# Both output projections of a hybrid decoder kernel by seven half-size block products (one level of Strassen)

## The chip, the cores and the metric

One core of one Trainium2 chip runs the whole program in one launch. The metric is device time in microseconds of that core; a profiled execution also gives a span from the first to the last instruction, which is a little shorter than its time. TensorE is called PE, VectorE DVE, ScalarE ACT, GpSimd POOL and SyncE SP; SP computes nothing here and only issues DMAs, in order.

## The reference, cut to what matters

Two layers work on x of 1024 tokens by 1024 channels. Each makes a y of 1024 tokens by 2048 channels and ends in an output projection with a 2048 by 1024 weight matrix, added to x:

```python
# layer 0 (even): two branches, concatenated to 2048 channels
y_a = u * sg.reshape(bsz, seq, A_WIDTH) * jax.nn.silu(za)
...
return jnp.concatenate([y_a, y_b], axis=-1) @ w_out
# layer 1 (odd): attention over 16 heads, 2048 channels
o = o.reshape(bsz, seq, C_WIDTH) * jax.nn.silu(z)
return o @ w_out
# trunk
x = x + even_layer(...); x = x + odd_layer(...)
return rmsnorm(x, final_g)
```

## The kernel before

All products keep float32 accuracy by splitting both operands: `split2` makes a high part in fp32r (ACT casts it) and a low part (DVE subtracts), and each block product is three matmuls, high-high, high-low and low-high. `fetch_w` loads a weight chunk of 128 by 1024 (512 KB) on SP's queue into one of two buffers `wr`, `split_w` makes `wh` and `wl` of it, also two buffers each.

The order of the program: normalisation and gates; the gMLP stage (`gmlp`), in which group after group g = 0 to 7 takes a `u` weight chunk, 48 matmuls of 128x512 and eight small `sp` matmuls, and then eight `za` groups of 48 matmuls; the mLSTM heads (`mlstm`); the output projection of layer 0; the second layer's attention, 16 heads; the output projection of layer 1; the final normalisation. The finished gMLP rows `yu` go to DRAM (`yd`) from POOL's queue. A Tile scheduler orders each engine's instructions from this program, with its buffers and their reuse; each queue then runs in its own order.

An output projection has 16 blocks of 128 channels (kb) by 8 tiles of 128 tokens. y comes from DRAM (`yd` in layer 0, `wd` in layer 1, where it is multiplied by `rr`, the rows of inverse norms, first) into `wout_y`. Columns 0 to 511 are made first in eight PSUM tiles, two from `unit` (named un) and six named wps, by 128x512 matmuls: 16 x 8 x 3 = 384 a layer. Then `wout_rest` makes columns 512 to 767 and 768 to 1023, each by 384 matmuls of 128x256, while the earlier columns are added to the residual `xa`, squared for the norm (ACT) and multiplied by the gain `gB` (POOL, L344). The last piece is finished tile by tile.

`split_w` waits for a free pair wh, wl, so a weight load on SP can wait until PE has read the weights two chunks earlier; what stands behind it on SP waits too. In layer 1 the loads of y and rr stand on the same queue, and rr goes through two buffers `yr` that DVE must have read.

Of the kernel before, what the change touches and what calls it, by code (L numbers as in the profile page):

```python
# [35 lines left out]

Y0, PA = 4, 2
# [9 lines left out]
class Trunk:  # L47
# [106 lines left out]
    def run(self):  # L154
        tc, nc, io = self.tc, self.nc, self.io
        with tc.tile_pool(name="const", bufs=1) as cp, \
# [6 lines left out]
            self.x2 = dp.tile([NT, P, D], F32, name="x2d")  # L163
            self.wp = tc.alloc_tile_pool(name="weights", bufs=1)
# [8 lines left out]
            run(self.wout_part(range(2, 8), 0, Y0))  # L173
# [4 lines left out]
            q = pool("wout0c")  # L178
            self.wout_y(q, Y0, 8, wy)
            self.wout_y(p, 8, 16, wy)  # L180
            run(self.wout_part(range(8), Y0, 16))
            rest = self.wout_rest(p)
            next(rest)
            q.release()
            wy.release()

# [4 lines left out]
            for t in range(NT):  # L191
                next(rest)
                if t >= 2:
                    self.to_feature(self.xa[t - 2], t - 2, *((self.psum, "S", 2) if t >= 6 else ()))
            ps = [self.unit() for _ in range(2)]
            self.proj_half(w, ps[0], 0)
            self.to_feature(self.xa[6], 6, self.psum, "C", 2)
# [7 lines left out]
            self.to_feature(self.xa[7], 7, self.psum, "C", 2)  # L205
# [11 lines left out]
            for h in range(CH):  # L217
                att = self.odd_head(odd, h)
                for i in range(NT):
                    if i in SLOTS.get(h, range(NT)):  # L220
                        next(fill, None)
                        left -= 1
                        if left == 0:
                            hT.release()
                            wy = pool("wout1a")
                            self.wout_start(1)
                            self.wout_y(wy, 0, PA, wy)
                            self.wout_ps(range(2))
                            fill = self.wout_part(range(2), 0, PA)
                    next(att)  # L230
            self.odd_tail(odd, CH - 1)
            run(fill)
            self.wout_y(wy, PA, 7, wy)
            self.wout_ps(range(2, 8))
            run(self.wout_part(range(2, 8), 0, PA))
            run(self.wout_part(range(8), PA, 7))
# [18 lines left out]
    def wout_start(self, layer):  # L255
        self.layer = layer
        self.yh, self.yl, self.ysplit = [], [], []
        self.wsrc = self.io["wF"] if layer == 0 else self.io["wG"]
        self.wps = [None] * NT

    def wout_ps(self, ts_):

        t1 = lambda tag, n=1, w=512: self.psum.tile([P, w], F32, name="wps", tag=tag, bufs=n)
        for t in ts_:
            if t < 2:
                self.wps[t] = self.unit()
            elif self.layer == 0:
                self.wps[t] = t1(*{2: ("S", 2), 3: ("S", 2), 4: ("C", 2), 5: ("C", 2), 6: ("N",), 7: ("o",)}[t])
            elif t >= 6:
                self.wps[t] = t1("tp" if t == 6 else "O")  # L270
            elif t % 2 == 0:
                two = t1("S", 2, T)
                self.wps[t], self.wps[t + 1] = two[:, :512], two[:, 512:]

    def wout_y(self, pool, lo, hi, raws):

        nc = self.nc
        if self.layer == 1 and raws is pool:
            pool.tile([P, T], F32, name="yr", tag="yr", bufs=2)
        for kb in range(lo, hi):  # L280
            self.yh.append(pool.tile([P, T], F32R, name=f"yh{kb}"))
            self.yl.append(pool.tile([P, T], F32R, name=f"yl{kb}"))
        for kb in range(lo, hi):
            raw = self.yl[kb].bitcast(F32)
            ld = nc.sync.dma_start(out=raw, in_=(self.y if self.layer == 0 else self.w)[kb])
            if self.layer == 1:
                o, raw = raw, raws.tile([P, T], F32, name="yr", tag="yr", bufs=2)
                nc.sync.dma_start(out=raw, in_=self.rr[kb:kb + 1].broadcast_to([P, T]))
                nc.vector.tensor_tensor(out=raw, in0=o, in1=raw, op=ALU.mult)
            self.ysplit.append((ld.ins, *self.split2(self.yh[kb], self.yl[kb], raw)))  # L290

    def wout_mm(self, ps, kb, t, wh, wl):
        sl = slice(t * P, (t + 1) * P)
        for n, (a, b) in enumerate(((self.yh, wh), (self.yh, wl), (self.yl, wh))):
            self.nc.tensor.matmul(out=ps, lhsT=a[kb][:, sl], rhs=b, start=(kb == 0 and n == 0), stop=(kb == 15 and n == 2))  # L295

    def wout_part(self, ts_, lo, hi):

        for i in range(lo // 2, (hi + 1) // 2):
            w = self.fetch_w(self.wsrc[i])  # L300
            with self.after(*(self.ysplit[2 * i - 1][1:] if i else ())):
                wh, wl = (a.rearrange("p (k c) -> p k c", k=2) for a in self.split_w(w))
            for kb in range(max(lo, 2 * i), min(hi, 2 * i + 2)):
                for t in ts_:
                    self.wout_mm(self.wps[t], kb, t, wh[:, kb % 2, :], wl[:, kb % 2, :])
                yield
# [913 lines left out]
```

## Time and profile before

| what | value |
|---|---|
| median of 3 runs | 2156.04 us (2155.82 to 2158.85) |
| the profiled execution | 2155.46 us |
| its span | 2153.7 us |
| PE busy | 2122.1 us (99%) |
| DVE, ACT, POOL busy | 1375.5, 943.5, 188.7 us |
| DMA moved | 233.65 MB, mean 108 GB/s |
| mean granted clock of PE | 0.997 |

The time of a run is the span and 1.76 us around it. PE has work nearly all the time, so the time goes where PE's instructions go, and what another engine or queue does counts when PE then waits. The rows that matter stand further down.

### The profile page before, as it was taken

Reading aid. Unit: us, or ns where it says so; the run is one execution under the profiler, and the core shown is the slowest. Engines: PE = TensorE matmul, PEld = TensorE weight load, DVE = VectorE, ACT = ScalarE, POOL = GpSimd, SP = SyncE. Lnnn points to the kernel's source line nnn. Section 1 sums busy time; section 2 is a strip of 40 time slices with the busy share of each in tenths; the row PEclk is TensorE's granted clock in tenths of the full one; section 3 lists DMA queues with packets and bytes.
Section 4 is the critical chain, followed back from the end, with each engine's and each line's share of the span. In section 5 each row is a group of like instructions: output and inputs, shape, how many; then the busy total and the mean of one; then the engine's idle time right before and its main releaser. Section 6 shows DMA issues by size and latency. Waiting matters only on the chain.

```text
span 2153.7 us, 33782 instructions
## 1 busy us (share of the span) xinstructions
PE 2122.1 (99%) x12554; PEld 1858.8 (86%) x12554; DVE 1375.5 (64%) x3117; ACT 943.5 (44%) x1907; POOL 188.7 (9%) x315
## 2 busy tenths in 40 slices
PE   8899999999999999999999999999999999998998
PEld 7888889898989889988888888888888888887898
DVE  6352225767677622648777777777877777898525
ACT  5511214343434312335555555555555555665222
POOL 0000000000000000301111111110111011111002
PEclk9999999999999999999999999999999999999999
DMA  4311222111122441255444444444444443336812
GB/s 172 118 40 40 71 87 74 50 64 64 54 70 99 163 170 69 97 144 135 126 111 110 112 112 125 117 109 112 110 112 121 125 108 105 104 85 217 301 50 89
DMA packets 89337, 233.65 MB, mean 108 GB/s; under 512 B 19109, under 2 KB 20037, under 8 KB 89173
## 3 DMA queue, kind: packets, MB, share of 16 engines
q1 hardware_dynamic: 74420, 194.65, 29.7%
q0 software_dynamic: 14752, 36.85, 5.6%
q8 instruction: 99, 1.62, 0.3%
q14 instruction: 66, 0.53, 0.1%
HBM read 136.86 MB, written 27.43 MB: 76 GB/s over the span
## 4 chain that ended last, share of the span: by engine, by line
PE 84%; DVE 5%; DMA 3%; issue 3%; ACT 2%; SPq 2%; POOL 1%; DVEq 0%; POOLq 0%; ACTq 0%
PE un L135 38%; PE wps L295 11%; PE un L150 5%; PE S L558 5%; PE ops L150 4%; PE un L295 3%; PE O L604 3%; PE tp L590 3%; PE xps L135 2%; PE N L941 1%; PE O L605 1%; DMA sw<-xs 1%; PE vps L913 1%; PE dC L941 1%; SPq L451 1%
## 5 line engine op out<-in xcount | busy, mean ns | idle before, releaser
L135 PE MATMUL un<-hh,wh 128*128 128x512 f32 x1240 | 490.2, 395 | 1.2 <-ACT xs L437 1.2
L135 PE MATMUL un<-hh,wl 128*128 128x512 f32 x1240 | 490.2, 396 | 1.0 <-DVE wl L97 0.9
L135 PE MATMUL un<-hl,wh 128*128 128x512 f32 x1240 | 486.9, 393 | 0.0
L97 DVE TENSOR_TENSOR wl<-wr,wh 128x1024 fp32r<-128x1024 f32 (+1 forms) x163 | 205.4, 1261 | 315.2 <-ACT wh L96 283.6
L96 ACT CAST wh<-wr 128x1024 fp32r<-128x1024 f32 (+1 forms) x163 | 170.8, 1049 | 384.5 <-PE un L135 178.0
L135 PEld LDWEIGHTS un<-hh,wl 128*128 128x128 f32 x1240 | 233.0, 188 | 52.2 <-DVE wl L97 3.4
L135 PEld LDWEIGHTS un<-hh,wh 128*128 128x128 f32 x1240 | 233.4, 188 | 46.9 <-ACT xs L437 1.5
L135 PEld LDWEIGHTS un<-hl,wh 128*128 128x128 f32 x1240 | 233.1, 188 | 47.3
L566 ACT ACTIVATE p<-p,mn 128x128 f32<-128x128 f32 (+7 forms) x256 | 197.8, 774 | 122.7 <-DVE mn L563 122.5
L563 DVE CUSTOM_DVE_ANT_0 p<-S,mask 128x128 f32<-128x128 f32 (+7 forms) x256 | 184.9, 751 | 2.2 <-PE tp L590 1.7
L295 PE MATMUL wps<-wh,yh 128*128 128x256 f32 (+1 forms) x576 | 184.2, 321 | 0.2 <-ACT wps L323 0.2
L295 PE MATMUL wps<-wl,yh 128*128 128x256 f32 (+1 forms) x576 | 183.4, 319 | 0.0
L295 PE MATMUL wps<-wh,yl 128*128 128x256 f32 (+1 forms) x576 | 183.4, 319 | 0.0
L150 PE MATMUL un<-wh,hh 128*128 128x256 f32 (+1 forms) x560 | 160.3, 287 | 4.1 <-ACT wh L96 2.6
L150 PE MATMUL un<-wl,hh 128*128 128x256 f32 (+1 forms) x560 | 159.4, 285 | 1.4 <-DVE wl L97 1.4
L150 PE MATMUL un<-wh,hl 128*128 128x256 f32 (+1 forms) x560 | 159.2, 284 | 0.2 <-DVE hl L97 0.2
L97 DVE TENSOR_TENSOR PT<-tp,PT 128x512 fp32r<-128x512 f32 (+1 forms) x192 | 106.1, 553 | 30.4 <-ACT PT L96 30.2
L295 PEld LDWEIGHTS wps<-wh,yh 128*128 128x128 f32 x576 | 109.2, 190 | 9.4 <-ACT wps L323 0.8
L295 PEld LDWEIGHTS wps<-wh,yl 128*128 128x128 f32 x576 | 109.3, 190 | 7.6
L295 PEld LDWEIGHTS wps<-wl,yh 128*128 128x128 f32 x576 | 109.4, 190 | 7.4
L604 PE MATMUL O<-PT,Vh 128*128 128x512 f32 x320 | 113.6, 388 | 0.1
L96 ACT CAST PT<-tp 128x512 fp32r<-128x512 f32 (+1 forms) x192 | 91.6, 477 | 47.4 <-PE tp L590 44.9
(324 smaller groups left out, 4393.5 us busy)
## 6 DMA issues: line engine op xcount, KB each, us to landing
wr<-wO SPq DMA_DIRECT2D x79, 512.0 KB
wr<-wE SPq DMA_DIRECT2D x46, 512.0 KB
sw<-xs SPq DMA_DIRECT2D x256, 64.0 KB
Qh<-xh SPq DMA_DIRECT2D x128, 128.0 KB
Ql<-xl POOLq DMA_DIRECT2D x128, 128.0 KB, 4.0
wr<-wF SPq DMA_DIRECT2D x18, 512.0 KB
wr<-wG SPq DMA_DIRECT2D x18, 512.0 KB
yl<-yd SPq DMA_DIRECT2D x16, 512.0 KB
```

What stands on the lines that cost most here:

```text
L96: return (self.nc.scalar.copy(out=out_h, in_=src).ins, self.nc.vector.tensor_tensor(out=out_l, in0=src, in1=out_h.bitcast(F32), op=ALU.sub ...
L97: self.nc.vector.tensor_tensor(out=out_l, in0=src, in1=out_h.bitcast(F32), op=ALU.subtract).ins)
L135: nc.tensor.matmul(out=ps, lhsT=a[:, kb, :], rhs=b[:, kb, :], start=(kb == 0 and i == 0), stop=(kb == KB - 1 and i == 2))
L150: nc.tensor.matmul(out=ps, lhsT=a[:, k0 + k, sl], rhs=b, start=start and k == i == 0, stop=stop and k == n - 1 and i == 2)
L295: self.nc.tensor.matmul(out=ps, lhsT=a[kb][:, sl], rhs=b, start=(kb == 0 and n == 0), stop=(kb == 15 and n == 2))
L451: q.dma_start(out=dst[a:a + 64].bitcast(F32), in_=src[64 * c:64 * c + 64].bitcast(F32))
L558: mm(out=Ss[c][:, lo:lo + n], lhsT=Q2[c][qt // 4][i][:, qs], rhs=K2[c][lo // 512][:, :n], start=i == 0, stop=i == 1)
L563: nc.vector.tensor_tensor_reduce(out=p[:, :W], in0=S[:, :W], in1=self.mask[:, T - W:], scale=-0.125, scalar=1e30, op0=ALU.add, op1=ALU.min ...
L566: nc.scalar.activation(out=p[:, :W], in_=p[:, :W], func=AF.Exp, scale=-1.0, bias=mn, accum_out=s)
L590: self.nc.tensor.transpose(out=tp[:, i, :], in_=p[:, s0:s0 + P], identity=self.ident)
L604: mm(out=O.rearrange("p (a t) -> p a t", a=2)[:, :, a0:], lhsT=Vh, rhs=pt, start=s == 0, stop=False)
L941: mm(out=out, lhsT=lhsT[a], rhs=rhs[b], start=first and i == 0, stop=last and i == 2)
```

## The change

Both projections are made with 2 by 2 blocks: y in four blocks of 512 tokens by 1024 channels, the weights in four blocks of 1024 channels by 512 columns, and the Winograd form of Strassen's method, seven products of such blocks instead of eight. Four of the products need sums of the weights' blocks. `wout_sums` makes them in the gMLP stage, behind the odd u groups for layer 0 and behind the odd za groups for layer 1: eight calls, each with four loads of 512 KB on SP's queue into the tiles wb0 to wb3, which have one buffer each, four POOL operations of 128x1024, and four stores of 512 KB to DRAM (`td`) on POOL's queue.

The order of the products is 1, 7, 2, 6, 5, 3, 4. `wout_load` brings y in pairs of channel blocks and halves of the tokens (a000 is half 0, channels' half 0, pair 0); in layer 1 each pair also takes two broadcast loads of rr and a DVE multiplication. `wout_lhs` makes the sums of y's blocks on POOL (s3 for product 7, further sums for 6 and 3). Each product is 4 pairs x 2 x 4 token tiles x 3 = 96 matmuls of 128x512. Product 1 belongs to both token halves: ACT copies it to p1, and POOL adds p1 to the residual tiles (`wout_p1`). Products 1, 2, 5, 3 accumulate in one set of four PSUM tiles, 7, 6, 4 in the other; `wout_evac` adds them to xa. No 128x256 matmul is left in the projections.

```diff
+    def wout_sums(self, pool, layer, i):
+        b11, b12, b21, b22 = (pool.tile([P, 1024], F32, name=f"wb{j}", tag=f"wb{j}") for j in range(4))
+        t2 = pool.tile([P, 1024], F32, name="wt2", tag="wt2")
+        for j, b in enumerate((b11, b12, b22, b21)):
+            nc.sync.dma_start(out=b, in_=self.io["wF" if layer == 0 else "wG"][4 * (0, 1, 3, 2)[j] + i])
+        g = nc.gpsimd.tensor_tensor
+        g(out=b11, in0=b12, in1=b11, op=sub)
+        g(out=t2, in0=b22, in1=b11, op=sub)
+        g(out=b12, in0=b22, in1=b12, op=sub)
+        g(out=b21, in0=b21, in1=t2, op=sub)
+        for j, b in enumerate((b11, t2, b12, b21)):
+            nc.gpsimd.dma_start(out=self.td[layer][j][i], in_=b)
...
+    def wout_lhs(self, n, i):
+        if n == 7:
+            s3 = self.ytmp.tile([P, 2, 512], F32, name="s3", tag="t3", bufs=2)
+            g(out=s3, in0=a11, in1=a21, op=sub)
+            return s3
+        if n == 6:
+            g(out=a21, in0=a21, in1=a22, op=ALU.add)
+            g(out=a11, in0=a21, in1=a11, op=sub)
+        if n == 3:
+            g(out=a12, in0=a12, in1=a11, op=sub)
+        return {1: a11, 2: a12, 3: a12, 4: a22, 5: a21, 6: a11}[n]
...
+    def wout_prod(self, n, tiles=range(4), groups=((0,), (1,), (2,), (3,))):
+        for grp in groups:
+            for i in grp:
+                w = self.load_w(self.wsrc[n][i])
+                parts.append((i, self.split_y(self.wout_lhs(n, i)), [a.rearrange("p (k c) -> p k c", k=2) for a in w]))
+            for t in tiles:
+                for i, y, w in parts:
+                    for k in range(2):
+                        for j, (a, b) in enumerate(((0, 0), (0, 1), (1, 0))):
+                            self.nc.tensor.matmul(out=self.wps[x, t], lhsT=y[a][:, k, t * P:(t + 1) * P], rhs=w[b][:, k, :],
...
+    def wout_p1(self):
+        for t in range(4):
+            x = self.xa[t + 4].rearrange("p (a c) -> p a c", a=2)
+            g(out=x, in0=x, in1=self.p1[t].unsqueeze(1).broadcast_to([P, 2, 512]), op=add)
+            x = self.xa[t][:, 512:]
+            g(out=x, in0=x, in1=self.p1[t], op=add)
```

In the program, layer 0 now runs product 1 for tiles 0 and 1 in the last mLSTM head, then tiles 2 and 3, `wout_rest`, `wout_p1`, the other loads, product 7 and so on. Layer 1 runs product 1 for tiles 0 and 1 as filler in the attention, then product 7, then product 1 for tiles 2 and 3, then `wout_p1`, the loads of the second half of y's channels, and the rest:

```diff
+            self.wout_ps(range(4), "B")
+            run(self.wout_prod(7))
+            self.wout_ps((2, 3), "A")
+            run(self.wout_prod(1, (2, 3)))
             odd.release()
             self.xp = pool("x3acc", side="right")
             p = pool("wout1b")
...
+            self.wout_rest(p)
+            self.wout_p1()
+            self.wout_evac(7)
+            for i in range(4):
+                for k in range(2):
+                    self.wout_load(p, k, 1, (i,))
+            for n in (2, 6, 5, 3):
+                run(self.wout_prod(n))
```

What this does to the queues is shown at three places. On SP's queue in the gMLP stage the kernel before has only the weight loads of the groups; these are those of u7, za0, za1, za2 and za3:

```order
L74 DMA wr_2037<-wE 128x1024
L74 DMA wr_2115<-wE 128x1024
L74 DMA wr_2178<-wE 128x1024
L74 DMA wr_2241<-wE 128x1024
L74 DMA wr_2304<-wE 128x1024
```

With the change the same weights, u7 (2099), za0 (2194), za1 (2257) and za2 (2337), stand between the loads of the last two calls of `wout_sums`:

```order
L72 DMA wr_2099<-wE 128x1024
L290 DMA wb3_2609<-wG 128x1024
L290 DMA wb0_2606<-wG 128x1024
L290 DMA wb1_2607<-wG 128x1024
L72 DMA wr_2194<-wE 128x1024
L290 DMA wb2_2608<-wG 128x1024
L290 DMA wb3_2752<-wG 128x1024
L290 DMA wb0_2749<-wG 128x1024
L290 DMA wb1_2750<-wG 128x1024
L72 DMA wr_2257<-wE 128x1024
L290 DMA wb2_2751<-wG 128x1024
L72 DMA wr_2337<-wE 128x1024
```

A load of wb1 for a new call waits for the store that still reads wb1 of the call before, so za0 stands behind such a wait of call 6 (counted from 0) and za1 behind one of call 7; before, nothing but weights stood ahead of them.

On POOL's queue after the last mLSTM head the kernel before issues the last two stores of y and then has nothing before the multiplications by the gain:

```order
L1042 DMA yd14_79<-xc_5987 128x512
L1042 DMA yd15_80<-xc_6068 128x512
L344 ISA
L344 TENSOR_TENSOR xa0_7549<-xa0_7549,gB_7565 128x768
L344 TENSOR_TENSOR xa1_7550<-xa1_7550,gB_7565 128x768
```

With the change the additions of p1 to the residual tiles stand there, then the two stores, and behind them the sums s3 that product 7 reads (the two additions for tiles 4 and 0 stand ahead of these rows):

```order
L398 TENSOR_TENSOR xa5_7379<-xa5_7379,p1_7104 128x1024
L400 TENSOR_TENSOR xa1_7375<-xa1_7375,p1_7104 128x512
L398 TENSOR_TENSOR xa6_7380<-xa6_7380,p1_7344 128x1024
L400 TENSOR_TENSOR xa2_7376<-xa2_7376,p1_7344 128x512
L398 TENSOR_TENSOR xa7_7381<-xa7_7381,p1_7352 128x1024
L400 TENSOR_TENSOR xa3_7377<-xa3_7377,p1_7352 128x512
L1118 DMA yd14_79<-xc_6135 128x512
L1118 DMA yd15_80<-xc_6216 128x512
L338 TENSOR_TENSOR s3_7429<-a000_6499,a100_7362 128x1024
L338 TENSOR_TENSOR s3_7465<-a001_6502,a101_7365 128x1024
```

The additions for tiles 6, 2, 7 and 3 wait for product 1 of token tiles 2 and 3, so s3 has moved behind the end of product 1.

On SP's queue in layer 1 the kernel before alternates loads of y and rr with weight loads:

```order
L285 DMA yl13_21008<-wd13_8838 128x1024
L288 DMA yr_20940<-rrd_8841 128x1024
L285 DMA yl14_21040<-wd14_8839 128x1024
L288 DMA yr_20972<-rrd_8841 128x1024
L74 DMA wr_21047<-wG 128x1024
L285 DMA yl15_21078<-wd15_8840 128x1024
L288 DMA yr_21010<-rrd_8841 128x1024
L74 DMA wr_21109<-wG 128x1024
```

With the change the whole second half of y's channels, eight pairs of which these are the last two, stands ahead of the first weights of product 2 (20863):

```order
L324 DMA a013_20849<-wd14_8642 128x512
L324 DMA a013_20849<-wd15_8643 128x512
L329 DMA yr_20852<-rrd_8644 128x512 x2
L324 DMA a113_20856<-wd14_8642 128x512
L324 DMA a113_20856<-wd15_8643 128x512
L329 DMA yr_20859<-rrd_8644 128x512 x2
L72 DMA wr_20863<-wG 128x1024
L72 DMA wr_20897<-wG 128x1024
L72 DMA wr_20931<-wG 128x1024
```

The weights of product 2 have moved behind 32 loads of 256 KB, which themselves stand behind the last weights of product 1.

## Rows read from the trace of the kernel before

**Rows 1.** The page: the span, then busy time, share and instructions of engines.
```profile
span 2153.7 us, 33782 instructions
...
PE 2122.1 (99%) x12554; PEld 1858.8 (86%) x12554; DVE 1375.5 (64%) x3117; ACT 943.5 (44%) x1907; POOL 188.7 (9%) x315
```

**Rows 2.** Chain of waits, layer 0: start us, us, engine, tile, line, matmuls.
```profile
780.95 4.20 PE wps L295 x18
785.15 1.40 PE un L295 x6
...
816.89 2.16 PE wps L295 x18
819.05 0.72 PE un L295 x6
```

**Rows 3.** Chain of waits, layer 1, same columns.
```profile
2021.01 4.08 PE wps L295 x18
2025.09 1.36 PE un L295 x6
```

**Rows 4.** ScalarE in order of time, gMLP stage: start, duration, line, operation.
```profile
229.39 1.05 ACT L96 CAST wh<-wr 128x1024 fp32r<-128x1024 f32 x1 [5.66 <-PE un L135]
...
241.47 1.05 ACT L96 CAST wh<-wr 128x1024 fp32r<-128x1024 f32 x1 [4.77 <-PE un L135]
```

**Rows 5.** SyncE queue in order of time: DMA issues, merged.
```profile
102.22 51.98 SPq L74 DMA_DIRECT2D wr<-wE  x6
```

**Rows 6.** All engines in order of time, around one weight load.
```profile
152.62 1.23 DVE L97 TENSOR_TENSOR wl<-wr,wh 128x1024 fp32r<-128x1024 f32 x1 [4.89 <-PE sp L1113]
...
153.88 0.33 SPq L74 DMA_DIRECT2D wr<-wE  x1
```

**Rows 7.** DMA, 153.5 to 157 us: GB/s in 40 equal slices.
```profile
GB/s 0 0 0 0 0 0 0 0 0 0 0 0 0 0 0 234 234 94 140 234 187 328 234 655 234 468 328 374 374 421 468 234 328 328 47 47 0 0 0 0
```

**Rows 8.** DMA, 244 to 250 us: GB/s in slices; issues, KB, us to landing.
```profile
GB/s 0 0 0 0 0 246 164 137 164 246 437 410 410 410 328 382 246 273 410 437 437 410 437 410 300 246 28 27 0 0 0 0 0 0 0 0 0 0 0 0
...
yd<-yu POOLq DMA_DIRECT2D x1, 512.0 KB, 3.9
```

**Rows 9.** Tile yd: its stores by operation, duration ns min/median/max.
```profile
L1130 POOL DMA_DIRECT2D yd<-yu x8: 533/533/533, 244.7 to 323.1; - x8
```

**Rows 10.** Line L344: duration ns min/median/max, first and last start, shapes.
```profile
L344 POOL TENSOR_TENSOR xa<-xa,gB x16: 1847/1858/2843, 859.3 to 2110.9; 128x768 f32<-128x768 f32 x16
```

**Rows 11.** GpSimd in order of time, 858 to 876 us.
```profile
859.26 16.56 POOL L344 TENSOR_TENSOR xa<-xa,gB 128x768 f32<-128x768 f32 x8 [117.42 <-DMA x2d<-xa]
```

**Rows 12.** VectorE in order of time, 858 to 876 us.
```profile
861.18 1.78 DVE L346 TENSOR_SCALAR pre<-pre 128x8 f32<-128x8 f32 x1
862.88 2.96 DVE L97 TENSOR_TENSOR wl<-wr,wh 128x1024 fp32r<-128x1024 f32 x1
871.41 2.69 DVE L97 TENSOR_TENSOR wl<-wr,wh 128x1024 fp32r<-128x1024 f32 x1 [5.58 <-ACT wh L96]
```

**Rows 13.** Windows: busy us (instructions) of PE, PEld, DVE, ACT, POOL; clock; DMA; GB/s.
```profile
126.00:230.00 104.00, 103.70 (x512) 85.76 (x511) 39.99 (x63) 17.53 (x25) 0.00 (x0) 1.00 0.12 41
...
1950.00:1972.00 22.00, 18.06 (x85) 14.10 (x86) 20.13 (x43) 13.41 (x32) 2.15 (x4) 0.92 0.89 321
1972.00:2055.00 83.00, 81.89 (x371) 67.49 (x370) 49.66 (x61) 27.27 (x36) 1.56 (x3) 1.00 0.66 242
```

**Rows 14.** The same view in short stretches around the end of attention.
```profile
1950.00:1955.00 5.00, 3.76 (x15) 3.33 (x16) 3.45 (x9) 2.76 (x8) 0.00 (x0) 0.68 0.94 288
...
1970.00:1972.00 2.00, 2.00 (x12) 1.66 (x11) 1.98 (x3) 1.13 (x3) 0.17 (x1) 1.00 1.01 408
```

**Rows 15.** SyncE queue in order of time, from the first load of layer 1's products.
```profile
1948.70 0.33 SPq L285 DMA_DIRECT2D yl<-wd  x1
```

**Rows 16.** TensorE in order of time, the last matmuls of attention.
```profile
1974.13 0.39 PE L627 MATMUL O<-sqh,ones 128*128 128x256 f32 x1 [1.09 <-DVE sql L97]
```

**Rows 17.** Windows at the end of the kernel, columns as in group 13.
```profile
2145.60:2153.70 8.10, 0.19 (x2) 0.00 (x0) 3.65 (x17) 2.27 (x4) 0.00 (x0) 0.76 0.49 194
```

More of the change, by code (lines that the diff above doesn't have):

```diff
@@ L163, in run @@
             self.x2 = dp.tile([NT, P, D], F32, name="x2d")
+            self.td = [[dp.tile([4, P, 1024], F32, name=f"td{l}{j}") for j in range(4)] for l in range(2)]
             self.wp = tc.alloc_tile_pool(name="weights", bufs=1)
@@ L232, in run @@
             run(fill)
[L233 to L236, printed above, removed]
+            self.wout_ps(range(4), "B")
+            run(self.wout_prod(7))
+            self.wout_ps((2, 3), "A")
+            run(self.wout_prod(1, (2, 3)))
             odd.release()
@@ L277, in wout_y, with wout_load @@
+    def wout_load(self, pool, half, k, pairs):
         nc = self.nc
[L278 to L285, printed above, removed]
-            if self.layer == 1:
[L287 to L305, printed above, removed]
+        hs = slice(half * 512, (half + 1) * 512)
@@ new lines, in wout_load @@
+        for i in pairs:
+            x = self.a[half, k, i] = pool.tile([P, 2, 512], F32, name=f"a{half}{k}{i}")
+            for n in range(2):
+                nc.sync.dma_start(out=x[:, n], in_=(self.y if self.layer == 0 else self.w)[8 * k + 2 * i + n][:, hs])
+            if self.layer == 1:
+                r = self.ytmp.tile([P, 2, 512], F32, name="yr", tag="t3", bufs=2)
+                for n in range(2):
+                    kb = 8 * k + 2 * i + n
+                    nc.sync.dma_start(out=r[:, n], in_=self.rr[kb:kb + 1, hs].broadcast_to([P, 512]))
+                nc.vector.tensor_tensor(out=x, in0=x, in1=r, op=ALU.mult)
@@ L310, in wout_rest @@
         nc, io, layer = self.nc, self.io, self.layer
+        self.yp.append(pool)
+        self.np = pool
+        self.ytmp = pool if layer == 0 else self.ytmp
         res = io["x"].rearrange("(t p) d -> t p d", p=P) if layer == 0 else self.x2
-        xa = self.xa = [self.xp.tile([P, D], F32, name=f"xa{t}") for t in range(NT)]
-        with self.after(self.ysplit[7][0]):
-            for t in range(NT):
-                nc.sync.dma_start(out=xa[t], in_=res[t])
-        gB = pool.tile([P, D], F32, name="gB")
@@ new lines, in wout_evac @@
+    def wout_evac(self, n, tiles=range(4)):
+        nc, xa = self.nc, self.xa
+        v = nc.vector.tensor_tensor
+        lo, hi = slice(0, 512), slice(512, D)
+        for t in tiles:
+            ps = self.wps["A" if n in (2, 5, 3) else "B", t]
+            if n in (7, 6):
+                v(out=xa[t][:, hi], in0=xa[t][:, hi], in1=ps, op=ALU.subtract if n == 7 else ALU.add)
+                if n == 6:
+                    v(out=xa[t + 4][:, hi], in0=xa[t + 4][:, hi], in1=ps, op=ALU.add)
+                continue
+            u, c = {2: (t, lo), 5: (t + 4, hi), 3: (t, hi), 4: (t + 4, lo)}[n]
+            x = xa[u][:, c]
+            v(out=x, in0=x, in1=ps, op=ALU.add)
+            if n == 5:
+                ps = self.yp[0].tile([P, 512], F32, name="sqj", tag="p1", bufs=4)
+            nc.scalar.activation(out=ps, in_=x, func=AF.Square, accum_out=self.ss[:, u, c.start // 512:c.start // 512 + 1])
+            if self.layer == 0:
+                (nc.sync if n in (2, 5) else nc.gpsimd).dma_start(out=self.x2[u][:, c], in_=x)
+            if n in (2, 5):
+                nc.gpsimd.tensor_tensor(out=x, in0=x, in1=self.gB[:, c], op=ALU.mult)
@@ L1100, in gmlp @@
         yp = new_pool("yA", side="right")
+        wsp = new_pool("w_sums", side="right")
         yu = []
```

196 lines of the change are left out of this document (103 added, 93 removed).

## The prediction

> **What bounds the kernel now.** I read the page first: PE is busy 2122.1 of 2153.7 us [rows 1]. So the kernel is bound by the number and pace of matmuls, and an edit elsewhere counts only where it makes PE wait. Then the chain of waits in the two projections, which gives the pace. In layer 0, 24 matmuls of 128x512 take 4.20 + 1.40 us, 0.2333 each, and 24 of 128x256 take 2.16 + 0.72, 0.120 each [rows 2]; in layer 1 the wide ones take 4.08 + 1.36, 0.2267 each [rows 3]. A 128x256 matmul therefore costs slightly more than half a wide one. Then I read, at the three places where the queues change, what a load, a store and a POOL operation last, and how much time the present order leaves.
>
> **1. Matmuls.** Before, a layer has 384 wide and 768 narrow ones: layer 0, 384 x 0.2333 + 768 x 0.120 = 89.6 + 92.2 = 181.8 us; layer 1, 87.1 + 92.2 = 179.2. After, it has 7 x 96 = 672 wide ones: 156.8 and 152.3. That is -25.0 and -26.9, together **-51.9 us**. All of it is on the path, since PE is. Everything below is what is given back.
>
> **2. The sums in the gMLP stage.** POOL is idle there (0.00 us in 104) and DMA moves 41 GB/s [rows 13], so the work itself has room: 32 operations and 32 MB. The question is the order on SP. The wb tiles have one buffer, so the calls form a ring: load wb1, four POOL operations, issue the stores, the store of wb1 lands, load wb1 again. A 128x768 POOL operation takes 1858 ns [rows 10]; by size 128x1024 is 2.48 us, four are 9.9. A load of 512 KB goes out at 153.88 and its last bytes move in the slice that ends at 156.7, 2.75 us [rows 6, 7]. Two stores are issued ahead of wb1's at 0.53 us each [rows 9], and a store takes 3.9 us to land with one load beside it [rows 8]. That is 2.75 + 9.9 + 1.1 + 3.9 = 17.6 us a call at least. Dearer: three stores of a call fly together, and at about 0.33 MB per us, which two transfers got there (1.05 MB in some 3.2 us [rows 8]), each further one adds 1.6; so 5.5 to land, 4.35 for a load beside the fourth store, and POOL at the mean of its eight contested operations, 16.56/8 x 4/3 = 2.76 us [rows 11], 11.0 for four: 22 us. I take the middle, 20.
>
> Call 0's loads follow u0's weights, issued at 102.22 [rows 5]. wb1 is the third of them with u1's weights between: landed about 109; four operations to 119, stores to about 126. za1's weights stand behind wb1 of call 7, which is free six rings later: 126 + 6 x 20 = 246, landed 249. Before, their cast starts at 241.47, with PE on the end of the group before it [rows 4]. So PE waits 7.5 us. za0 (five rings, 226, landed 229) just meets its cast at 229.39. The wait begins at a ring of (241.47 - 2.75 - 126)/6 = 18.8 us; at 17.6 it is 0, at 22 it is 19, and if POOL's first operation is slow as well, 26. Term: **+7.5** (0 to 26). After za1 nothing of weight waits for a store of the sums.
>
> **3. Layer 0, from product 1 to product 7.** Product 7 reads s3. On POOL it stands behind the additions for tiles 6, 2, 7 and 3, which need the end of product 1. From that end: ACT copies p1 (half the cast of 1.05 [rows 4], 0.5), two times 1024 and 512 elements 2 x (2.48 + 1.24) = 7.4, two store issues 1.07, s3 2.48, the cast of s3 1.05: 12.5 us in which PE has nothing. It could start 1.4 us sooner (tile 2 ends six matmuls before tile 3), and at POOL's contested 2.76 take 14 to 16. Term: **+12.5** (11 to 16). The load of a100, behind product 7's fourth weights, needs about 7 us from there and is covered by POOL. Product 2's weights follow some 5 MB of loads, 15 us, and product 7 covers them.
>
> **4. Layer 1, start of product 7.** The first y load goes out at 1948.70 [rows 15]. Ahead of product 7's weights stand eight pairs with their rr, 8.4 MB, and 1.05 MB of weights. This sort of load got 321 GB/s there [rows 13]: 29 us, so 1979 with the first latency and 1980 with the cast. PE finishes the last squares at 1974.5 [rows 16] and has 12 matmuls of product 1 left: 1977.2. Term: **+4** (0 to 7); product 7 starts near 1981.
>
> **5. Layer 1, product 2.** Product 7 takes 96 x 0.2267 = 21.8, so to 2003, and product 1 for tiles 2 and 3 10.9 more, to 2014. The last weights of product 1 wait for a wr buffer, which is read when wh and wl come free at product 7's end, 1.05 + 1.23 us [rows 4, 6] after 2003: 2005. Behind them stand the 8.4 MB of the second half, then product 2's own 0.5 MB. At 321 GB/s that is 28 us, with latency and cast 2035: PE waits **+21**. At the fastest stretch, 408 GB/s [rows 14], it is 2029, a wait of 15; at the mean of the stretch where DVE throttled the same loads through two yr buffers, 242 GB/s [rows 13], 2044, 30. The page "DMA: Bandwidth & Descriptors" of the Trainium skill (Specifications) gives about 358 GB/s as the HBM limit of a core; by it the wait would be 18 us. The 408 here goes above it for 2 us, the 321 over 22 us does not.
>
> **6. DVE beside POOL.** The subtraction wl of 128x1024 takes 1.23 us [rows 6]; the two that fell among POOL's eight operations took 2.96 and 2.69, and one on eight columns 1.78 [rows 11, 12]. In a product DVE makes two such subtractions per 24 matmuls: 2.5 us of 5.44, but 5.65 if both are stretched, 0.2 over. POOL runs 16 such operations and 16 of 512 columns a layer, about 60 us, ten of 28 pairs: 2 us a layer at most, some of it behind the waits above. Term: **+3** for both (0 to 10). The page "SBUF — State Buffer" of the Trainium skill (SBUF: two separate sides) says that such a DVE operation and a POOL one exclude each other for the whole instruction. The trace agrees: 1.73 and 1.46 us too many, under POOL's 1.86. By the rule alone two full waits of 2.48 a pair would make 7.4 us, 2 over: 20 a layer. The two rows had no such full wait, so the sum stays with them.
>
> **7. Clock.** After an idle time the granted clock was 0.68 for five us, with PE busy 3.76 [rows 14]: 0.32 x 3.76 = 1.2 us lost. Four long waits: **+5** (0 to 6). The end keeps its steps, 8.1 us [rows 17]: 0.
>
> **Sum.** -51.9 + 7.5 + 12.5 + 4 + 21 + 3 + 5 = +1.1. The profiled execution took 2155.46, 1.76 more than its span, so 2156.6; the median is 0.6 above that execution, so **2157 us**. A measurement of this kernel tells about 0.2%, 4.3 us, from no change: the forecast is that almost all of the matmul gain is given back in waits.
>
> **The rivals.** *Layer 1's second half comes in time* (the faster side). SP is free to run ahead if the split of product 1's third weights is scheduled or freed earlier than 2005; the loads have no other wait than two yr buffers. Each us that they start sooner is a us less. With the wait at 15, 2150; without it, 2157 - 21 - 1.2 = 2135. It decides when product 2's first weights land before about 2025. For it: 408 GB/s was reached; against it: 321 over the longer stretch.
>
> *The ring of the sums is slow* (the slower side). At 23 us a ring, za1 comes at 126 + 138 + 2.75 = 267, 25.5 late, and the time is 2175. For it: six transfers per call are in flight at once, and DVE is busy 40 of 104 us against POOL [rows 13]; against it: the store of 3.9 us already had a load beside it. It decides from 20.7 us a ring, where the wait is 11.5.
>
> *The port binds the products.* If nearly every split among POOL's operations waits, DVE falls behind PE and the time is 2157 + 7 to + 20, so 2164 to 2177. Against it: half of a layer's POOL operations stand beside a wait of PE that exists anyhow.
>
> **How the numbers follow.** Forecast 0.40, spread 10 us either way by the bounds of terms 2 and 5: faster 0.11, same 0.16, slower 0.13. Loads in time 0.25, all faster. Slow ring 0.23, slower. Port 0.12: same 0.02, slower 0.10. So faster 0.36, same 0.18, slower 0.46. The range goes from the middle of the faster case, 2135, to near the end of the slow ring, 2180; the forecast's own is 2147 to 2167.
>
> **What would show it.** Right: a PE gap before the za1 group with the releaser on a wr load and wb loads on SP ahead of it; a gap of some 12 us after product 1 of layer 0 with POOL full; one of some 20 us after product 1 of layer 1 while DMA is above 0.8. Wide matmuls at 0.227 to 0.233 show term 1. Wrong: rings of 17 or of 25 us, a POOL operation of 128x1024 far from 2.5, or matmuls whose pace falls because the splits come late.

## The result and the profile after

The changed kernel takes **2244.86 us** (2242.28 to 2249.3) against 2155.93 in the same runs: a ratio of 1.0412, 95% interval 1.0391 to 1.0433. The forecast was 2157, at most 2180. The profiled execution, the slowest of the four, has a span of 2247.5 us, 93.8 more than before; every difference below is one of spans. Its page answers to [rows 1]:

```profile
span 2247.5 us, 32307 instructions
...
PE 2103.8 (94%) x11594; PEld 1803.5 (80%) x11594; DVE 1537.3 (68%) x3113; ACT 998.0 (44%) x1943; POOL 415.6 (18%) x427
```

The matmuls that were to go are gone: 12554 - 11594 = 960, which is 2 x (1152 - 672). By term 1 PE's busy time should fall by 51.9 to 2070.2. It is 2103.8, so the remaining matmuls run 33.6 us longer than at the pace of before, and PE now stands idle for 2247.5 - 2103.8 = 143.7 us where it stood 31.6. That is the whole account: -51.9 + 33.6 + 112.1 = +93.8.

Windows show where. Columns as in [rows 13]: stretch, length, busy us (instructions) of PE, PEld, DVE, ACT, POOL, then granted clock, DMA share, GB/s:

```profile
100.00:150.00 50.00, 40.92 (x242) 36.69 (x243) 33.26 (x49) 9.13 (x18) 24.31 (x16) 0.80 0.65 235
200.00:250.00 50.00, 42.84 (x193) 35.00 (x193) 20.40 (x15) 6.21 (x9) 30.85 (x19) 0.92 0.55 192
...
750.00:800.00 50.00, 33.91 (x149) 26.51 (x147) 43.90 (x74) 18.55 (x27) 18.70 (x12) 0.81 0.50 175
800.00:850.00 50.00, 34.36 (x121) 26.64 (x121) 35.52 (x16) 12.25 (x13) 41.71 (x14) 0.75 0.51 182
2000.00:2050.00 50.00, 33.38 (x130) 25.63 (x129) 44.26 (x78) 23.87 (x50) 13.21 (x11) 0.76 0.69 221
2050.00:2100.00 50.00, 30.77 (x132) 24.12 (x130) 35.88 (x27) 15.26 (x16) 30.27 (x13) 0.85 0.76 262
2100.00:2150.00 50.00, 28.89 (x115) 23.04 (x116) 34.32 (x21) 14.74 (x20) 34.54 (x14) 0.74 0.39 127
```

The clock of 0.74 to 0.92 is a mean of the levels 1.2 and 2.4 GHz over each window, idle time included; in the stretches of [rows 13] before, it was 0.92 to 1.00. In each row PE is 7 to 21 us short of its 50.

The times at which named matmuls first or last start cut the span into parts (S and dC are tiles of the attention and the mLSTM heads; lengths in us):

| part, from one mark to the next | before | after | difference | forecast, clock apart |
|---|---|---|---|---|
| start to the first dC matmul (gMLP) | 368.3 | 402.5 | +34.2 | +7.5 |
| to the first S matmul (mLSTM, layer 0's projection) | 596.7 | 617.6 | +20.9 | -25.0 + 12.5 + 1.5 = -11.0 |
| to the last S matmul (attention) | 996.7 | 995.3 | -1.4 | 0 |
| to the last wps matmul (layer 1's projection) | 183.8 | 222.7 | +38.9 | -26.9 + 4 + 21 + 1.5 = -0.4 |
| to the end | 8.2 | 9.4 | +1.2 | 0 |

All three places that the prediction named are dearer than forecast, by 27 to 39 us each; the forecast's 5 us for the clock are in none of the rows, while the longer matmuls are in these three differences.

**The gMLP stage.** SP's queue in order of time, from the weights of u7 on; "x4" are issues merged into one row, and its time is that from the first issue to the end of the last, waits included:

```profile
206.36 12.53 SPq L290 DMA_DIRECT2D wb<-wG  x4
218.99 0.38 SPq L72 DMA_DIRECT2D wr<-wE  x1
228.77 9.42 SPq L290 DMA_DIRECT2D wb<-wG  x3
238.24 0.49 SPq L72 DMA_DIRECT2D wr<-wE  x1
240.09 20.23 SPq L290 DMA_DIRECT2D wb<-wG  x4
260.37 0.51 SPq L72 DMA_DIRECT2D wr<-wE  x1
```

Counted against the order shown ahead of the prediction (u7, three wb, za0, four wb, za1), the three wr are u7, za0 and za1: each goes out right behind the wb that waited for a store. ScalarE's casts, as in [rows 4]:

```profile
203.51 1.04 ACT L94 CAST wh<-wr 128x1024 fp32r<-128x1024 f32 x1 [5.66 <-PE un L133]
225.47 1.04 ACT L94 CAST wh<-wr 128x1024 fp32r<-128x1024 f32 x1 [14.64 <-DMA wr<-wE]
226.43 1.08 ACT L1187 ACTIVATE u<-un 128x512 f32<-128x512 f32 x2
244.43 1.04 ACT L94 CAST wh<-wr 128x1024 fp32r<-128x1024 f32 x1 [16.92 <-DMA wr<-wE]
266.76 1.04 ACT L94 CAST wh<-wr 128x1024 fp32r<-128x1024 f32 x1 [20.30 <-DMA wr<-wE]
275.81 1.05 ACT L94 CAST wh<-wr 128x1024 fp32r<-128x1024 f32 x1 [5.60 <-PE un L133]
```

The casts that wait for a DMA are those of u7, za0 and za1, each 6.2 to 6.5 us behind its issue; the last row is za2's. So in the kernel before, where the same casts follow each other, 241.47 [rows 4] is za2's and 229.39 is za1's. The row of L1187 is the evacuation of the group in work (ScalarE reads its finished sum `un`), which stands on ScalarE's queue right behind the cast that waited. The ring itself, by the first operation of each call (its line, then the stores' landing):

```profile
L292 POOL TENSOR_TENSOR wb<-wb,wb x8: 2339/2374/2402, 112.1 to 265.6; 128x1024 f32<-128x1024 f32 x8
```
```profile
DMA to landing us min/median/max: 2.9/5.4/7.7
```

(265.6 - 112.1)/7 = 21.9 us a ring, and 5.4 us for a store of 512 KB to land.

**The products.** GpSimd in order of time, in layer 0 at the sums that product 6 reads, while TensorE is still in product 7:

```profile
825.11 3.39 POOL L341 TENSOR_TENSOR a<-a,a 128x1024 f32<-128x1024 f32 x1
828.58 3.26 POOL L342 TENSOR_TENSOR a<-a,a 128x1024 f32<-128x1024 f32 x1
831.81 3.31 POOL L341 TENSOR_TENSOR a<-a,a 128x1024 f32<-128x1024 f32 x1
835.21 3.25 POOL L342 TENSOR_TENSOR a<-a,a 128x1024 f32<-128x1024 f32 x1
```

VectorE in the same stretch:

```profile
822.80 3.43 DVE L95 TENSOR_TENSOR wl<-wr,wh 128x1024 fp32r<-128x1024 f32 x1
826.15 6.78 DVE L95 TENSOR_TENSOR yl<-a,yh 128x1024 fp32r<-128x1024 f32 x2
832.85 3.36 DVE L95 TENSOR_TENSOR wl<-wr,wh 128x1024 fp32r<-128x1024 f32 x1
836.14 3.40 DVE L95 TENSOR_TENSOR yl<-a,yh 128x1024 fp32r<-128x1024 f32 x1
```

They take turns: one POOL operation and one DVE subtraction every 3.35 us, where alone the one takes 2.37 (the row of L292 above) and the other 1.23 [rows 6]. A pair of weights and y needs two subtractions, 6.7 us, and its 24 matmuls are done in 5.44 [rows 3]. The waits for late splits (wl and yl) of TensorE in the products are 22.0 us in all.

**The long waits.** TensorE's waits by what ended them (us in total, times, longest), and then the two longest gaps in order of time:

```profile
PE un L366 <- ACT wh L94: 39.2, 2, 34.3
PE wps L366 <- ACT yh L94: 15.1, 1, 15.1
PE un L133 <- ACT u L1187: 14.5, 3, 7.3
```
```profile
810.28 0.80 PE L366 MATMUL wps<-wh,yh 128*128 128x512 f32 x1 [15.10 <-ACT yh L94]
...
2116.86 1.22 PE L366 MATMUL un<-wh,yh 128*128 128x512 f32 x2 [34.32 <-ACT wh L94]
```

The first is the start of product 7 in layer 0 (behind 6.4 us of smaller gaps since the end of product 1), the second that of product 2 in layer 1; its weights went out at 2110.04, behind the second half of y, whose loads began at 2072.66:

```profile
2072.66 0.91 SPq L324 DMA_DIRECT2D a<-wd  x2
...
2110.04 0.85 SPq L72 DMA_DIRECT2D wr<-wG  x2
```

### The profile page after: what moved, and what is told of

It reads as the page before. It is cut to its first block, busy times and chain, and to the rows that moved or that the text cites. A ratio compares the mean times of both kernels' runs of the same rounds, so it can differ in the third digit from the quotient of the medians.

```text
span 2247.5 us, 32307 instructions
## 1 busy us (share of the span) xinstructions
PE 2103.8 (94%) x11594; PEld 1803.5 (80%) x11594; DVE 1537.3 (68%) x3113; ACT 998.0 (44%) x1943; POOL 415.6 (18%) x427
## 2 busy tenths in 40 slices
DMA packets 109749, 281.81 MB, mean 125 GB/s; under 512 B 21348, under 2 KB 22276, under 8 KB 109588
## 5 line engine op out<-in xcount | busy, mean ns | idle before, releaser
L133 PE MATMUL un<-hh,wh 128*128 128x512 f32 x1240 | 493.8, 398 | 15.7 <-ACT u L1187 14.5
L95 DVE TENSOR_TENSOR wl<-wr,wh 128x1024 fp32r<-128x1024 f32 (+1 forms) x191 | 262.1, 1374 | 207.3 <-ACT wh L94 197.8
L94 ACT CAST wh<-wr 128x1024 fp32r<-128x1024 f32 (+1 forms) x191 | 199.8, 1048 | 283.2 <-PE un L133 174.7
L366 PE MATMUL wps<-wh,yh 128*128 128x512 f32 x320 | 128.3, 406 | 18.2 <-ACT yh L94 15.1
L366 PE MATMUL wps<-wl,yh 128*128 128x512 f32 x320 | 129.8, 406 | 9.2 <-DVE wl L95 9.0
L95 DVE TENSOR_TENSOR yl<-a,yh 128x1024 fp32r<-128x1024 f32 x56 | 85.1, 1521 | 70.3 <-ACT yh L94 70.1
L94 ACT CAST yh<-a 128x1024 fp32r<-128x1024 f32 x56 | 58.6, 1047 | 165.6 <-PE wps L366 130.7
L694 POOL DMA_DIRECT2D wd<-wt x64 | 36.7, 574 | 510.2 <-DVE wt L692 485.6
L366 PE MATMUL wps<-wh,yl 128*128 128x512 f32 x320 | 128.7, 403 | 1.1 <-DVE yl L95 1.1
L148 PEld LDWEIGHTS un<-wh,hh 128*128 128x128 f32 x560 | 108.4, 194 | 6.5 <-ACT wh L94 3.2
```

What stands on the lines that cost most here:

```text
L94: return (self.nc.scalar.copy(out=out_h, in_=src).ins, self.nc.vector.tensor_tensor(out=out_l, in0=src, in1=out_h.bitcast(F32), op=ALU.sub ...
L95: self.nc.vector.tensor_tensor(out=out_l, in0=src, in1=out_h.bitcast(F32), op=ALU.subtract).ins)
L133: nc.tensor.matmul(out=ps, lhsT=a[:, kb, :], rhs=b[:, kb, :], start=(kb == 0 and i == 0), stop=(kb == KB - 1 and i == 2))
L148: nc.tensor.matmul(out=ps, lhsT=a[:, k0 + k, sl], rhs=b, start=start and k == i == 0, stop=stop and k == n - 1 and i == 2)
L366: self.nc.tensor.matmul(out=self.wps[x, t], lhsT=y[a][:, k, t * P:(t + 1) * P], rhs=w[b][:, k, :], start=n in (1, 7, 5) and i == k == j == ...
L694: nc.gpsimd.dma_start(out=self.w[h][:, js], in_=wt)
```

## The experiments

Every ratio is against the kernel before, measured on the same chip in the same rounds.

### e1: the sums of y's blocks and the additions of p1 on DVE

```diff
-        g, sub = self.nc.gpsimd.tensor_tensor, ALU.subtract
+        g, sub = self.nc.vector.tensor_tensor, ALU.subtract
```

The same in `wout_p1` and in the multiplication by the gain. The sums of the weights stay on POOL.

> The sums of y's blocks, the additions of p1 and the multiplications by the gain are made on DVE instead of POOL in both projections; the gMLP stage is as in the change. Theory lock (POOL and DVE exclude each other, so that a pair of one POOL operation and one split takes 3.4 us): the splits fall back to 1.2 us, the gaps of PE in product 7 of layer 0 and ahead of product 2 of layer 1 shrink, 2200 to 2220 us. Theory order (only the places of loads on the queue count): the same gaps, within 6 us of 2245.

2210.1 us, ratio 1.0253 (1.0238 to 1.0269): 34.8 less than the change, within the 2200 to 2220 that the theory of turns ("lock") gave. DVE has POOL's part on top of its own and is yet busy for less in sum (1526.4 us against 1537.3), since each piece is short again:

```profile
807.83 1.22 DVE L341 TENSOR_TENSOR a<-a,a 128x1024 f32<-128x1024 f32 x1
808.97 1.22 DVE L95 TENSOR_TENSOR yl<-a,yh 128x1024 fp32r<-128x1024 f32 x1
```

Two operations in 2.27 us on one engine, against 3.35 on two. By the marks above, layer 0 takes 593.8 (617.6 in the change) and layer 1 210.4 (222.7), together 36.1 less; of the rest of the 40.5 between the two profiled executions 3.5 are in the gMLP stage, whose program is the same. TensorE's waits for late splits fall from 22.0 to 7.4, the wait of product 7 from 15.1 to 4.7 (7.6 for the last head's output gate `og` now stand before it, 5.6 in the change), that of product 2 in layer 1 only from 34.3 to 27.8. The edit takes away the turns and POOL's slower pace (2.37 us an operation alone, 1.22 on DVE) together. At the sums of product 6 the turns are what binds: two POOL operations alone would be 4.74 us a pair, less than the 5.44 of its matmuls. Elsewhere the two aren't separated.

### e2: no sums of the weights

The calls of `wout_sums` are taken out and products 4 to 7 read plain blocks of the weights, so the output isn't the reference's.

```diff
-                self.wout_sums(wsp, 0, g // 2)
+                pass
```

> No sums of the weights' blocks are made in the gMLP stage; products 4 to 7 read blocks of the weights as they are (so the output is not the reference's), with the same number and size of loads. Both theories: the first mLSTM matmul comes back from 402.5 to 368 us, and the time falls by about 34 us to 2211. If it falls by much less or more, part of the loss of the gMLP stage is given back or caused later.

2211.65 us, 1.0259 (1.0243 to 1.0274). The first dC matmul starts at 367.4 (before: 368.3), so the 34.2 us of the gMLP stage come from the sums; the two long waits of the projections stay (14.9 and 34.4).

### e3 and e4: the loads of the sums on POOL's queue; the sums on DVE

```diff
-            nc.sync.dma_start(out=b, in_=self.io["wF" if layer == 0 else "wG"][4 * (0, 1, 3, 2)[j] + i])
+            nc.gpsimd.dma_start(out=b, in_=self.io["wF" if layer == 0 else "wG"][4 * (0, 1, 3, 2)[j] + i])
```

e4 leaves the loads on SP and has `g = nc.vector.tensor_tensor` in `wout_sums`.

> The four loads of each call of the sums go out on POOL's queue instead of SP's; all arithmetic as in the change. Theory order: weights no longer stand behind waits of the sums, so only the late start of the u groups (some 10 to 13 us, DVE beside POOL) is left of the 34: about 2222 us. Theory lock alone: no change, 2240 to 2247.

> The sums of the weights' blocks are computed on DVE instead of POOL, their loads and stores stay where they are. Theory lock with order: the ring of a call shortens from 22 us to about 16, near the 16.8 at which no group waits, and the normalisation at the start is not stretched: 2210 to 2220 us. Rival: DVE waits for each call's loads in its own order and holds back the weights' splits behind it: 2245 or slower.

e3: 2217.1, 1.0286 (1.0271 to 1.0301); e4: 2220.17, 1.0294 (1.0277 to 1.0311). The first dC matmul starts at 376.4 and 376.8. With the loads off SP (e3) or the ring shortened by DVE's operations (e4, (225.5 - 113.3)/7 = 16.0 us a ring) no cast of these groups waits for a DMA any more, and PE sets their pace; in e3:

```profile
249.75 1.05 ACT L94 CAST wh<-wr 128x1024 fp32r<-128x1024 f32 x1 [4.77 <-PE un L133]
```

The casts tell where the 34 us arise. In the change 13.0 us are lost by the cast at 151.59 (138.57 before), no more are added up to u6's at 203.51 (190.47 before), and 21.3 come with the rings at u7, za0 and za1. In e3 the start costs 8.2 and nothing comes behind it, so the loads' place on SP's queue is worth the 21.3 and 4.8 of the start; PE still waits 5.3 us there for `av`. In e4 the start costs 3.2, and 5.5 come at u7 to za1, where PE waits 3.1 us for `yu`, which DVE makes.

### e5 to e8: the order in layer 1, then all together

In e5 (sums of y on POOL) and e6 (on DVE, as in e1) product 1 for tiles 2 and 3 and the first group of product 2 stand ahead of the other loads. e7 is e6 with the loads of e3. e8 is e7 with layer 0's product 7 ahead of `wout_p1` and a100 to a103 loaded on POOL's queue.

```diff
-            run(self.wout_prod(1, (2, 3)))
             odd.release()
...
+            self.wout_load(p, 0, 1, range(4))
+            run(self.wout_prod(1, (2, 3)))
+            two = self.wout_prod(2)
+            next(two)
             self.wout_rest(p)
             self.wout_p1()
             self.wout_evac(7)
+            next(two)
+            self.wout_load(p, 1, 1, range(4))
+            run(two)
```

> Layer 1 alone in another order: the pairs of half 0 of the second channels are loaded ahead of product 1 of tiles 2 and 3, product 2's first weights ahead of the residual rows, and the pairs of half 1 behind the second group of product 2; all arithmetic as in the change. Theory order: most of the 34 us that PE waits ahead of product 2 goes, 2213 to 2225 us. Rival (DVE, held by POOL, makes the multiplied pairs late wherever their loads stand): over 2238 us.

> The same order in layer 1, and the sums of y's blocks, the additions of p1 and the gains on DVE as in e1. If the two causes add: 2210 less 20 to 28, so 2182 to 2190 us. If they overlap (one wait seen twice): above 2195.

> As e6, and the loads of the weights' sums on POOL's queue as in e3. If the losses of the gMLP stage and of the projections are independent, it is 28 us faster than e6: 2154 to 2162 us, level with the kernel before. If what is saved early is lost later, less than 20 faster.

> As e7, and in layer 0 the y blocks of product 7 are loaded on POOL's queue, which no weight's split holds, and the additions of p1 stand behind the sums and splits of product 7's first two groups. Theory: the three waits of PE between product 1 and product 7 there (7.6, 4.7 and 3.1 us in e1) shrink by 8 to 12 us: 2143 to 2153, faster than the kernel before. Rival: DVE, which now has the additions inside product 7, is the bound there, and the time stays within 4 us of e7.

| run | us | ratio (interval) |
|---|---|---|
| e5 | 2241.03 | 1.0390 (1.0372 to 1.0407) |
| e6 | 2197.3 | 1.0193 (1.0178 to 1.0208) |
| e7 | 2173.72 | 1.0078 (1.0060 to 1.0095) |
| e8 | 2169.89 | 1.0061 (1.0037 to 1.0084) |

All four are slower than their forecasts. The rivals of e5 (over 2238), e6 (above 2195) and e8 (within 4 us of e7) came in by the number; e7 is 23.6 faster than e6, between its forecast (28) and its rival (less than 20). The runs of e7 and e8 overlap. The theory that the order of the loads is what costs layer 1 its time fell with e5: the waits for wh go from 39.2 to 17.9 and 6.5, those for wl from 20.1 to 26.3, and the time moves by 3.8. With the turns gone the same order is worth 12.8 (e1 to e6), still half of the forecast. So the sums of y on DVE are worth 43.7 with the new order (e5 to e6) and 34.8 without it: the two losses lie in part behind one another. e7 takes most of the 27.8 of e3 once more. In e8 a wait of 14.3 us stands in layer 0, since the new loads on POOL's queue stand behind the last two stores of y; the reason that its rival gave, DVE as the bound there, isn't what the trace shows.

### e9: layer 1 without rr

e8 without the loads of rr and the multiplications by it, so the output isn't the reference's.

```diff
-                nc.vector.tensor_tensor(out=x, in0=x, in1=r, op=ALU.mult)
```

> This is the kernel of e8 without layer 1's loads of rr and the multiplications of y by it, so that the output isn't the reference's. e8 was at 2169.9 us, and its layer 1 takes 16 us more than the kernel before from the last head's scores on, although its matmuls there should save 26.9: about 40 us of waits and slow clock remain. Theory 'volume': 16.8 MB of y and rr must come in over a queue that the multiplications throttle through two yr buffers; without rr half of these bytes and the throttle are gone, so 20 to 28 us less, 2142 to 2150. Rival 'order': the waits are those of splits and weight buffers behind each other and stay; 2163 to 2172.

2138.28 us, 0.9928 (0.9901 to 0.9956), 31.6 less than e8 and 4 below its forecast range. Layer 1 by the marks takes 177.8 us: 199.6 in e8, 183.8 before. These 21.8 are within the 20 to 28 that were expected; they are for the bytes of rr, the throttle of the two yr buffers and DVE's multiplications together, which this run doesn't separate. Of the other 13.0 us of the profiled executions 8.6 are in the gMLP stage (first dC matmul at 368.2 against 376.8), whose program is the same in both (the av operations met POOL's sums less: seven of them took 7.22 us), and 5.0 in the attention, where the first loads of y and rr go out; layer 0 takes 0.6 more. The first product windows of layer 1, in e8 and then in e9:

```profile
2000.00:2050.00 50.00, 41.31 (x165) 31.87 (x164) 40.85 (x46) 19.16 (x20) 0.49 (x1) 0.90 0.86 305
2050.00:2100.00 50.00, 42.34 (x178) 34.10 (x177) 43.96 (x46) 18.77 (x24) 0.00 (x0) 0.93 0.40 127
```
```profile
2000.00:2050.00 50.00, 43.98 (x177) 33.55 (x176) 48.01 (x50) 20.85 (x28) 0.00 (x0) 0.97 0.62 228
2050.00:2100.00 50.00, 50.00 (x219) 40.75 (x218) 30.98 (x35) 20.79 (x28) 0.00 (x0) 1.00 0.29 95
```

In the first window e8 moves 305 GB/s and PE is short of work. The last row is the pace of products with nothing in their way: 50.00/219 = 0.228 us a wide matmul, as term 1 took it.

### e10 and e11: the sums held back; Strassen in layer 0 alone

Both wait with the first sum until the first gated rows are there, and load a100 to a103 on SP ahead of product 7's weights with the additions of p1 behind its third group. e11 has layer 1 as in the kernel before and four calls of sums instead of eight.

```diff
+        if i == 0 and gate is not None:
+            nc.gpsimd.tensor_copy(out=b11[:, :1], in_=gate[:, :1])
```

> This is e8 with two more edits: the first POOL operation of the sums waits until yu1 is there, so that it doesn't stand beside the DVE operations av at the start of the gMLP stage (e8 still loses 8.5 us there); and in layer 0 the loads of a100 to a103 go to SP's queue ahead of product 7's weights, with the additions of p1 behind the third group of product 7 (e8 waits 14.3 us there). Theory, that each of these waits is what it looks like: 5 to 8 less in the gMLP stage and 8 to 13 less in layer 0, so 2149 to 2157, no different from the kernel before within 0.3%. Rival: the wait only moves to the next thing that is late (the splits of product 7, the weights of product 2); 2162 to 2170.

> Layer 0 as in e10, layer 1 as in the kernel before, and only the four calls of sums that layer 0 needs. If the gain of layer 0 (25.0 us of matmuls) is kept but for 1 to 4 in the gMLP stage and some 8 to 12 of waits and slow clock, the time is 2155.9 - 25 + 13 = 2140 to 2148, faster than the kernel before by 0.4 to 0.7%. Rival: layer 0's waits are moved and not removed, as in e8, where the layer kept 5 of 25: 2152 to 2156, no difference.

e10: 2175.17, 1.0093 (1.0078 to 1.0108), not better than e8, and slower than both its forecast and its rival, which was nearer. The eight `av` operations are back at their own length (below), but the eight calls now end near 333 us, and PE gets 11.16 of the 20 us after 340 at a clock of 0.67: the wait went to the other end of the stage. The first operation of the mLSTM heads on DVE waits for the landing of the sums' last store:

```profile
338.23 0.18 DVE L994 TENSOR_SCALAR vh<-ident 128x16 fp32r<-128x16 f32 x1 [12.60 <-DMA td<-wb]
```

ScalarE then waits 14.3 us for DVE, and PE between 343 and 360 for the weights' casts and splits. The two share no data; the kernel suggests that vh takes over room in SBUF that the sums had, which no run tests. The first dC matmul starts at 381.0, 4.2 later than in e8. Layer 0 takes 587.9, 3.7 less than in e8, instead of 8 to 13 less.

e11: **2147.88 us, 0.9965 (0.9953 to 0.9977)**, the one version that leaves nothing out and beats the kernel before, by 0.35%. Its first dC matmul starts at 365.7, so four sums held back cost nothing. The time is in the range that was expected, but in part by luck: layer 0 takes 591.2, 5.5 less than before, of the 25.0 that its matmuls give, as the rival said (5 of 25) and not the 13 to 17 of the forecast; the gMLP stage and the attention, each 2.6 shorter than before, make up for some of it. Of the 19.5 us that layer 0 gives back, half are in one place:

```profile
740.00:770.00 30.00, 20.14 (x76) 14.67 (x75) 23.69 (x39) 10.20 (x11) 1.08 (x2) 0.82 0.91 322
770.00:800.00 30.00, 29.98 (x125) 24.10 (x124) 29.32 (x31) 10.80 (x11) 0.00 (x0) 0.95 0.37 130
```

At 740 to 770 the DMA engines are 0.91 busy and PE lacks 9.9 us; ScalarE's casts wait there 4.5 us for weights and 6.2 for y. At the time when product 7 is due, y for it, the residual and the weights all have to come in.

## Why the prediction was wrong, by its steps

**1. Matmuls: right.** 960 fewer, at 0.228 us without waits.

**2. The sums: +34.2 instead of +7.5 (0 to 26).** The ring was sized rightly, at its dear end: 21.9 us with bounds of 17.6 and 22, and 5.4 to land with 5.5 in the dear case. Two things around it were wrong. In "Before, their cast starts at 241.47" the row is not za1's: the cast of a group stands a group ahead, the row is za2's, and za1's is 229.39, so the deadline was 12 us too late (in the same way 229.39 was taken for za0's). With the right one and the ring of 21.9, za1 lands at 126 + 6 x 21.9 + 2.75 = 260.2 and is 31 late. And the term counted only the group whose weights are late: it had nothing for what stands behind the waiting cast on ScalarE, the evacuation of the group in work, for which PE waited 14.5 us at the casts of u7, za0 and za1. Together the rings cost 21.3. The second loss, 13.0, lies at the start: the cast at 138.57 before comes at 151.59 with no ring wait ahead of it. Half of that is VectorE's eight single-input operations av, in the change, then before and in e10, where no sum stands beside them:

```profile
135.09 12.36 DVE L1174 TENSOR_SCALAR av<-av,amv,ar_y 128x1024 f32<-128x1024 f32 x8
```
```profile
131.05 5.87 DVE L1098 TENSOR_SCALAR av<-av,amv,ar_y 128x1024 f32<-128x1024 f32 x8
```
```profile
129.62 5.87 DVE L1187 TENSOR_SCALAR av<-av,amv,ar_y 128x1024 f32<-128x1024 f32 x8
```

The prediction had looked for POOL's slowing beside DVE there, not for DVE's. e2 shows that the sums are behind the 34.2, and e3 that the loads' place on SP's queue is behind the 21.3 and a part of the 13.0.

**3. Layer 0, product 1 to 7: 21.5 instead of 12.5 (11 to 16).** The longest wait, 15.1, is near the term, but the term was for all the time in which PE has nothing between the two products, and that is 21.5: the prediction had no place for the transposes of the last head's gate, which wait for `og` on DVE (5.6). POOL had ended its additions at 792.5; then it waited for the last rows of y to store them, and s3 for a100, which SP issued at 799.29, behind four loads of product 7's weights that held the queue for 21.53 us. "Covered by POOL" was wrong: the load was the last to come, and s3 waited 8.3 us for it.

**4. Layer 1, start of product 7: 7.5 instead of 4 (0 to 7), just over its bound.** It began 35.8 us after the first load of y (2002.77 to 2038.58), where the forecast had 32.3, from 1948.70 [rows 15] to near 1981, and PE waited 4.9 us for wh and 2.6 for wl there.

**5. Layer 1, product 2: 34.3 us and 4.2 for wl instead of 21 (15 to 30).** The mechanism is the one given: SP issues the loads of the second half from 2072.66 and product 2's weights at 2110.04. Two sizes were off. The loads began 34.1 us after product 7's start where the forecast had 24, since product 7 itself was slower. And 8.4 MB in 37.4 us are 224 GB/s, below the dear bound of 242: the yr buffers come free by DVE's multiplications, and one of these took up to 3.39 us beside POOL (1.22 alone). e1 gets 6.5 of the wait back, and e9, without rr, has 3.0 us of waits for wh left where e8, with the same order, has 21.3. So the order matters (e6), but behind it stand the loads and multiplications of rr.

**6. DVE beside POOL: the step that failed most, +3 (0 to 10), where e1 is 34.8 faster than the change.** It was read from two rows, 2.96 and 2.69 [rows 12], which fell among POOL operations by chance. At the sums of products 7 and 6 both engines have work waiting, and then they take strict turns. In the prediction's own terms PE waited 22.0 us for late splits (7.4 in e1), where 3 were put; the rest of the 34.8 is in the terms beside it, the waits ahead of product 7 and of product 2 and the clock. The rival "the port binds the products" named the condition, "if nearly every split among POOL's operations waits", and at these sums it held; its price of 7 to 20 was too low, most likely because it left those terms as they were, which no run takes apart. The page "SBUF — State Buffer" of the Trainium skill (SBUF: two separate sides) says that the pair of ports is taken for a whole instruction. The traces here agree, with one POOL operation to one DVE operation in 3.35 us, a little under the 3.60 that the two take alone; the prediction had put it aside for the two rows.

**7. Clock: 33.6 instead of 5 (0 to 6).** Four waits at 1.2 us each were counted from a single row [rows 14]. The waits are many more than four, and a long one costs more. Behind the 15.1 us ahead of product 7 the granted clock stays at 0.50, the level of 1.2 GHz, to near 818, and a wide matmul goes out every 0.43 us instead of 0.23:

```profile
814.00:816.00 2.00, 2.00 (x6) 1.55 (x5) 0.00 (x0) 0.00 (x0) 2.00 (x1) 0.50 1.06 381
```

PE is busy for 6.6 us at this level there, so some 3.3 are lost (an estimate from these windows). By the marks the 33.6 are spread: 12.7 in the gMLP stage, 9.6 to the first S, 12.7 in layer 1's projection, and 1.6 less in the attention. PE's busy time above 2070.2 is 33.6 in the change, 2089.1 - 2070.2 = 18.9 in e1, 2086.2 - 2070.2 = 16.0 in e2 and 2079.9 - 2070.2 = 9.7 in e9: it falls with the waits, though 6.6 of what e1 gives back are in the gMLP stage, which e1 doesn't change. That the clock is the whole of the 33.6 isn't shown.

Of the rivals, "layer 1's second half comes in time" didn't happen. The slow ring and the port both did, together, and each was priced as if it came alone; yet by their own prices 2157 + 18 + 20 = 2195 would still be 50 short. What stays open is how the 13 us at the start of the gMLP stage divide beyond av's 6.5 (the operation `ar_y` takes 2.1 longer, and 4.8 go with the loads' place on SP, which may overlap), and how e1's 34.8 divide between the turns and POOL's own pace.

## What to carry to other kernels

A kernel that is bound by matmuls pays for saved matmuls with work on the other engines: here with sums on POOL, more bytes (281.81 MB against 233.65) and loads that are due at the same time. Two engines that take turns, as DVE and POOL do here, are to be priced by the case that both have work queued, not by the rows where they met by chance. And before a queue's wait is set against a deadline, count which group the row of that deadline belongs to, and list what stands behind the waiting instruction on its own engine.

## What the runs showed of the hardware that was not expected

- POOL and DVE operations of 128x1024 with two inputs alternate one to one at 3.35 us a pair; both on DVE take 2.27 (e1).
- Single-input DVE operations are held too: eight av took 12.36 us beside the sums, 5.87 before and in e10.
- The matmuls themselves got longer by 33.6 us beside the idle time, in the gMLP stage and both projections; behind the wait of 15.1 us a wide one went out every 0.43 us at a granted clock of 0.50.
